# One PSUM pool from the projections to the end of attention, the first head's transposes inside the last gate block, roots shared by two token tiles, and `x` loaded ahead of the final additions

## The chip, the cores and the metric

The kernel runs on one core of one Trainium2 chip. TensorE (PE) does matmuls and transposes, VectorE (DVE), ScalarE (ACT) and GpSimd (POOL) the rest; SyncE (SP) and ScalarE issue the DMAs. The metric is the device time of one execution, in microseconds.

## The reference, cut to what matters

One layer of a hybrid encoder, sequence 1024, width 1024, batch 1, fp32. A Hyena branch (short convolution, two long convolutions with filters that a small MLP makes, 512 wide) and an attention branch (8 heads, 96 wide for q and k, 64 for v) are gated, added and multiplied by `w_out`:

```
h = rms_norm(x, g_norm); proj = h @ w_in
hy_in, z_hy, c_q, c_kv, k_rope, z_attn, gate_hy, gate_attn = split(proj)
v_h, x1, x2 = split(short_conv(hy_in))
k_spec = hyena_filter_spectra(...)          # sin(freq*(z @ w_f1 + b)), again with w_f2, then @ w_f3, decay, rfft
for o, gate in enumerate((x1, x2)):  zc = gate * long_conv(zc, k_spec[:, o], hy_bias[o])
u_hy = (zc * silu(z_hy)) @ w_hy_out
q = rms_norm(rms_norm(c_q) @ w_uq); kv = rms_norm(c_kv) @ w_ukv; k = rms_norm([k_nope, k_rope])   # rotary on 32 columns
u_attn = (softmax(q k^T / sqrt(96)) v * silu(z_attn)) @ w_attn_out
g_hy, g_at = split(sigmoid([gate_hy, gate_attn] + b_gate))
out = x + (g_hy * u_hy + g_at * u_attn) @ w_out
```

## The kernel before

Each fp32 product is made of three matmuls over operands split into a high and a low part (`hh`, `hl` are the two parts of the normalised input, transposed; `wh`, `wl` those of a weight block). The order of the instructions on each engine comes from a list scheduler of the framework with a cost model of its own; tiles come from pools with a number of buffers for each tag, and a tile that takes a buffer waits until the readers of the one before are done.

The stages, as TensorE goes through them: the startup (`build_hT`: transposes `ptx` of the normalised rows `xs`, in two halves of four row tiles, evacuated into `hh`, `hl`); the filter MLP (`pf`, with sines on ScalarE and many VectorE operations, two column halves); filter spectra (`pk`, `pu`) up to about 212 us; two long convolutions (`pu`, `pi`) up to about 605; `qkv` up to about 685; the last gate blocks up to 719; attention from there to 976 in 64 units (`S` scores, `pt` transposes of the exponentials `pr`, `pv` products with v); the two branch outputs (`hyena_out`, `pmo`); and the tail, the product with `w_out` in seven block products (`prod`, `po`) up to 1142.

Projections run all through this: 41 blocks of `proj_block`, each 48 matmuls `pm`, besides one of `proj_rope`; the scheduler lays them as fillers between the others. One block has two column halves of 512 in two PSUM banks (tag `mm`, 4 buffers), and each is evacuated by an instruction of its own: a sigmoid into `ob` for a gate (`fill_g`), copies for the latents (`fill_c`) and the short convolutions (`short_block`), sigmoid and product for `fill_z`. The PSUM pool `pp` closes before attention, whose scores, transposes and `pv` have pools of their own (`ssp`, `asp`).

`qkv` makes q, k and v for eight token tiles, two by two. For each tile it sums squares, takes a root with `rsqrt` (12 VectorE operations, three of them line L157), multiplies q and k by it, and stores them in DRAM (`qd`, `kdr`, `vd`); q and k have 4 buffers each. `load_pair` loads them back as `qr`, `kr`, `vr`, and the first head's 16 transposes (`pth`, function `prep`) turn them into `qh`, `ql`, `kh`, `kl`. Behind these loads in SP's queue stand five loads of `w_hy_out` tiles into `wr`, which ScalarE casts to `wh`.

In the tail, `finish(r, c, i, u, ps)` issues the load of an `x` tile (`xr`, 3 buffers), lets GpSimd add `u` (L1064), VectorE the product `ps` (L1065), and stores the tile; loads and stores of all 16 tiles stand in SP's queue in this order.

Of the kernel before, what the change touches and what calls it, by code (L numbers as in the profile page):

```python
# [34 lines left out]
CVB, MMB = 2, 4  # L35
# [58 lines left out]
class K:  # L94
# [106 lines left out]
    def build_hT(self, hp, xp):  # L201
# [6 lines left out]
        bank = lambda t: self.pp.tile([P, 512], F32, tag=t, bufs={"mm": MMB, "tp": 2, "cv": CVB}[t], name=self.nm("ptx"))  # L208
# [66 lines left out]
    def filter_mlp(self, fp, f1):  # L275
# [15 lines left out]
        for c in range(2):  # L291
            sl = slice(c * 512, (c + 1) * 512)
            self.split(z2[:, sl], zh[:, sl], zl[:, sl], after=self.half0)
            ps = self.pp.tile([P, 512], F32, tag="cv", bufs=CVB, name=self.nm("pf"))
            self.mm3(ps, w1h, w1l, zh[:, sl], zl[:, sl], True, True)
            x = self.sin_layer(f1, ps, fv[:, 0:1], fv[:, 1:2], 512)
            self.split(x, h1h[:, sl], h1l[:, sl])
        for c in range(2):
            sl = slice(c * 512, (c + 1) * 512)
            ps = self.pp.tile([P, 512], F32, tag="cv", bufs=CVB, name=self.nm("pf"))  # L300
# [27 lines left out]
    def filter_spectra(self, wk):  # L328
# [4 lines left out]
        for o in range(2):  # L333
            for hf in range(NHALF):
# [5 lines left out]
                for tp in range(4):  # L340
# [3 lines left out]
                    for d in range(2):  # L344
                        ps = self.pp.tile([P, 2, CW], F32, tag="cv", bufs=CVB, name=self.nm("pk"))
# [84 lines left out]
    def leaf_fwd(self, k, r, ch, cl, take):  # L430
# [5 lines left out]
        ps = self.pp.tile([P, 2, CW], F32, tag="cv", bufs=CVB, name=self.nm("pu"))  # L436
# [11 lines left out]
    def leaf_inv(self, k, p):  # L448
# [5 lines left out]
        ps = self.pp.tile([P, 2, CW], F32, tag="cv", bufs=CVB, name=self.nm("pi"))  # L454
# [97 lines left out]
    def proj_block(self, c0, m=P):  # L552

        nc, wp = self.nc, self.wp
        ps = [self.pp.tile([P, 512], F32, tag="mm", bufs=MMB, name=self.nm("pm")) for _ in range(2)]
        src = self.a["w_in"][0].rearrange("(d p) c -> p d c", p=P)
        for g in range(2):
# [5 lines left out]
            for i in range(4):  # L563
                d = 4 * g + i
                for (w, h, f) in ((wh, self.hh, 0), (wh, self.hl, 1), (wl, self.hh, 2)):
                    for c in range(2):
                        nc.tensor.matmul(ps[c][0:m], lhsT=w[:, i, 0:m], rhs=h[d][:, c * 512:(c + 1) * 512],  # L567
                                         start=(d == 0 and f == 0), stop=(d == 7 and f == 2))
        return ps

    def proj_rope(self, c0):

        nc, wp = self.nc, self.wp
        ps = [self.pp.tile([P, 512], F32, tag="mm", bufs=MMB, name=self.nm("pm")) for _ in range(2)]
# [6 lines left out]
        for d in range(8):  # L581
            for f, h in enumerate((self.hh, self.hl)):
                for c in range(2):
                    nc.tensor.matmul(ps[c][0:64], lhsT=w[:, d], rhs=h[d][:, c * 512:(c + 1) * 512],
                                     start=(d == 0 and f == 0), stop=(d == 7 and f == 1))
        return ps

    def short_block(self, blk, ps):
# [5 lines left out]
        for c in range(2):  # L594
            nc.scalar.copy(out=raw[:, 1 + c * 512:1 + (c + 1) * 512], in_=ps[c])
# [37 lines left out]
    def xz(self, b):  # L633
# [4 lines left out]
        for c in range(2):  # L638
            sl = slice(c * 512, (c + 1) * 512)
            nc.scalar.activation(out=sg[:, sl], in_=ps[c], func=AF.Sigmoid)  # L640
            nc.vector.tensor_tensor(out=sg[:, sl], in0=sg[:, sl], in1=ps[c], op=ALU.mult)
            nc.vector.tensor_tensor(out=acc[:, sl], in0=acc[:, sl], in1=sg[:, sl], op=ALU.mult)
# [4 lines left out]
    def fill_c(self, b):  # L647
# [4 lines left out]
        for c in range(2):  # L652
            nc.scalar.copy(out=ob[0:m, c * 512:(c + 1) * 512], in_=ps[c][0:m])
# [13 lines left out]
    def fill_z(self, b):  # L667
# [3 lines left out]
        for c in range(2):  # L671
            sl = slice(c * 512, (c + 1) * 512)
            nc.scalar.activation(out=ob[:, sl], in_=ps[c], func=AF.Sigmoid)
            nc.vector.tensor_tensor(out=ob[:, sl], in0=ob[:, sl], in1=ps[c], op=ALU.mult)
        nc.sync.dma_start(out=self.zaT[b], in_=ob)

    def fill_g(self, b):
        nc = self.nc
        ps = self.proj_block(3232 + b * P, P)
        ob = self.op.tile([P, L], F32, tag="ob", bufs=3, name=self.nm("ob"))  # L680
        for c in range(2):
            sl = slice(c * 512, (c + 1) * 512)
            nc.scalar.activation(out=ob[:, sl], in_=ps[c], func=AF.Sigmoid, bias=self.bg[:, b:b + 1])
# [9 lines left out]
    def convs(self, hf):  # L693
# [14 lines left out]
        for i in range(NB):  # L708
# [3 lines left out]
            for g in range(2):  # L712
                ps = self.pp.tile([P, 4, P], F32, tag="cv", bufs=CVB, name=self.nm("pty"))
# [7 lines left out]
    def qkv(self, kp):  # L721
# [56 lines left out]
        for hf in range(4):  # L778
            if hf < 3:
                C.update({(hf + 1, i): latent(hf + 1, i) for i in range(5)})  # L780
            ch, cl = [C[hf, i][0] for i in range(5)], [C[hf, i][1] for i in range(5)]
            for j in range(2):
# [55 lines left out]
    def attention(self, yp, wp, ssp, sp):  # L838
# [5 lines left out]
        rt = wp.tile([P, 512], F32R, tag="rT", name="rT")  # L844
        nc.gpsimd.memset(rt[64:P].bitcast(F32), 0.0)
        W = 2 * P

        def prep(h, j):
# [5 lines left out]
            if c == 0:  # L854
                QK[h, n] = [wp.tile([96, L], F32R, tag=n + x, bufs=2, name=self.nm(n + x)) for x in "hl"]
# [6 lines left out]
            if j == 3:  # L862
# [18 lines left out]
        def soft(u):  # L881
# [6 lines left out]
            pr = wp.tile([P, L], F32, tag="pr", bufs=2, name=self.nm("pr"))  # L888
# [376 lines left out]
```

## Time and profile before

| | |
|---|---|
| median of 3 runs | 1156.49 us (1154.57 to 1156.57) |
| profiled execution | 1155.32 us, span 1153.4 us |
| TensorE | busy 1099.4 us (95%), 5525 matmuls, mean granted clock 0.988 |
| VectorE, ScalarE, GpSimd | 893.0 (77%), 589.4 (51%), 107.3 us (9%) |
| chain that ended last | PE 65%, DVE 14%, DMA 10%, ACT 6%, issue 3% |

The span is the time from the first to the last instruction; 1.9 us of the execution lie outside it. A busy share is an average over all stages. The clock is the granted share of 2.4 GHz, 1.00 at full speed and 0.50 at 1.2 GHz, so that a mean between them is a mixture of the two. "Idle" in a row is the time that the engine waited just before, with what ended it.

### The profile page before, as it was taken

To read this page: it belongs to the slowest core of one execution; us is meant where nothing else is said; L and a number is where in the kernel's file an instruction comes from. 1 tells how busy PE (TensorE), PEld (TensorE's weight loads), DVE (VectorE), ACT (ScalarE), POOL (GpSimd) and SP (SyncE) were. 2 spreads that over 40 slices of the span, in tenths; PEclk is the share of its full clock that TensorE was granted. 3 is DMA by queue.
4 is the path that set the end of the run, shared out by engine and by line. 5 is a ranking of instruction groups with operands and counts; after the bars stand their busy time and mean duration, and the time that the engine had idled before them with its cause. 6 is when DMAs were issued, how large, how long until landed. Compare 5 with 4: busy or idle time off the path is not lost.

```text
span 1153.4 us, 15529 instructions
## 1 busy us (share of the span) xinstructions
PE 1099.4 (95%) x5525; PEld 909.7 (79%) x5525; DVE 893.0 (77%) x1631; ACT 589.4 (51%) x1101; POOL 107.3 (9%) x112
## 2 busy tenths in 40 slices
PE   4899999999999999999999999999999999999996
PEld 3678888888888888878887887787888887778874
DVE  6988788698788886778774893789788888478882
ACT  6745555754445434433433852777877776322420
POOL 0000000000000000000000132102200000250353
PEclk9989999999999999999999999899999999999998
DMA  5446444642335334334227557402202001896345
GB/s 212 133 146 198 155 163 174 205 119 65 89 91 147 105 115 128 91 88 127 91 83 233 148 154 248 146 29 74 92 25 77 1 20 50 274 298 217 91 128 182
DMA packets 119221, 150.27 MB, mean 130 GB/s; under 512 B 8548, under 2 KB 82408, under 8 KB 119144
## 3 DMA queue, kind: packets, MB, share of 16 engines
q1 hardware_dynamic: 107688, 120.97, 34.1%
q10 hardware_dynamic: 11456, 28.32, 6.6%
q8 instruction: 43, 0.70, 0.3%
q14 instruction: 34, 0.28, 0.1%
HBM read 101.81 MB, written 47.45 MB: 129 GB/s over the span
## 4 chain that ended last, share of the span: by engine, by line
PE 65%; DVE 14%; DMA 10%; ACT 6%; issue 3%; POOL 1%; SPq 0%; ACTq 0%; POOLq 0%; DVEq 0%
PE pm L567 33%; PE pu L128 8%; PE pt L903 4%; PE pi L128 4%; DMA wor<-in_w_out_dram 3%; PE S L119 2%; PE S L122 2%; PE S L121 2%; ACT pr L889 2%; PE pv L915 2%; PE pv L916 2%; DVE gg L988 1%; DMA out_dram<-xr 1%; DVE mo L139 1%; ACT PTh L138 1%
## 5 line engine op out<-in xcount | busy, mean ns | idle before, releaser
L567 PE MATMUL pm<-hh,wh 128*128 128x512 f32 x656 | 208.6, 393 | 1.8 <-DVE hl L143 0.9
L567 PE MATMUL pm<-hl,wh 128*128 128x512 f32 x656 | 208.9, 393 | 0.0
L567 PE MATMUL pm<-hh,wl 128*128 128x512 f32 x656 | 208.3, 392 | 0.1
L567 PEld LDWEIGHTS pm<-hh,wh 128*128 128x128 f32 x656 | 123.1, 189 | 27.7 <-DVE hl L143 1.1
L567 PEld LDWEIGHTS pm<-hh,wl 128*128 128x128 f32 x656 | 123.2, 188 | 26.0 <-DVE wl L139 0.5
L567 PEld LDWEIGHTS pm<-hl,wh 128*128 128x128 f32 x656 | 123.0, 188 | 25.3
L138 ACT CAST wh<-wr 128x512 fp32r<-128x512 f32 x98 | 60.3, 621 | 158.1 <-PE pm L567 107.7
L138 ACT CAST PTh<-pt 128x512 fp32r<-128x512 f32 x128 | 72.8, 587 | 41.1 <-PE pt L903 39.6
L139 DVE TENSOR_TENSOR PTl<-pt,PTh 128x512 fp32r<-128x512 f32 x128 | 83.8, 682 | 10.8 <-ACT PTh L138 10.2
L887 DVE TENSOR_REDUCE mx<-S 128x1 f32<-128x1024 f32 x64 | 77.9, 1217 | 13.2 <-PE S L122 13.1
L139 DVE TENSOR_TENSOR wl<-wr,wh 128x512 fp32r<-128x512 f32 x95 | 66.8, 708 | 15.7 <-ACT wh L138 15.4
L903 PE MATMUL pt<-ident,pr 128*128 128x128 f32 x512 | 75.9, 278 | 2.4 <-DVE PTl L139 1.4
L889 ACT ACTIVATE pr<-S,mx 128x1024 f32<-128x1024 f32 x64 | 71.8, 1121 | 7.0 <-DVE mx L887 6.6
L903 PEld LDWEIGHTS pt<-ident,pr 128*128 128x128 f32 x512 | 59.3, 142 | 18.2 <-DVE PTl L139 4.7
L915 PE MATMUL pv<-PTh,vc 128*128 128x256 f32 x256 | 69.1, 297 | 0.4 <-DVE at L926 0.4
L916 PE MATMUL pv<-PTl,vc 128*128 128x256 f32 x256 | 67.9, 293 | 0.0
L473 DVE TENSOR_TENSOR t<-pu,kt 128x512 f32<-128x512 f32 x64 | 41.0, 681 | 31.3 <-PE pu L128 30.7
L138 ACT CAST rh<-res 128x512 fp32r<-128x512 f32 x64 | 39.5, 619 | 41.8 <-PE pu L128 20.5
L119 PE MATMUL S<-kh,qh 96*128 96x512 f32 x128 | 54.5, 426 | 2.4 <-ACT pr L889 2.3
L121 PE MATMUL S<-kh,ql 96*128 96x512 f32 x128 | 53.5, 418 | 0.0
L122 PE MATMUL S<-kl,qh 96*128 96x512 f32 x128 | 52.5, 410 | 0.0
L915 PEld LDWEIGHTS pv<-PTh,vc 128*128 128x128 f32 x256 | 48.5, 189 | 4.7 <-DVE at L926 1.9
(285 smaller groups left out, 2391.2 us busy)
## 6 DMA issues: line engine op xcount, KB each, us to landing
wr<-in_w_in_dram SPq DMA_DIRECT2D x82, 256.0 KB, 3.2
wor<-in_w_out_dram SPq DMA_DIRECT2D x36, 256.0 KB, 4.7
dec<-in_dec_dram SPq DMA_DIRECT2D x16, 512.0 KB, 3.6
gT<-ob ACTq DMA_DIRECT2D x16, 512.0 KB, 2.9
gg<-gT SPq DMA_DIRECT2D x16, 512.0 KB, 4.4
kd<-kt ACTq DMA_DIRECT2D x28, 256.0 KB, 2.3
kt<-kd SPq DMA_DIRECT2D x28, 256.0 KB, 2.7
m<-gg ACTq DMA_DIRECT2D x16, 256.0 KB, 4.3
```

What stands on the lines that cost most here:

```text
L119: m = nc.tensor.matmul(out, lhsT=lh, rhs=rh, start=start, stop=False)
L121: nc.tensor.matmul(out, lhsT=ll, rhs=rh, start=False, stop=False)
L122: nc.tensor.matmul(out, lhsT=lh, rhs=rl, start=False, stop=stop)
L128: m = self.nc.tensor.matmul(out, lhsT=x, rhs=y, start=n == 0, stop=n == len(ops) - 1)
L138: self.behind(self.nc.scalar.copy(out=hi, in_=x), after)
L139: (eng or self.nc.vector).tensor_tensor(out=lo, in0=x, in1=hi.bitcast(F32), op=ALU.subtract)
L567: nc.tensor.matmul(ps[c][0:m], lhsT=w[:, i, 0:m], rhs=h[d][:, c * 512:(c + 1) * 512], start=(d == 0 and f == 0), stop=(d == 7 and f == 2))
L887: nc.vector.tensor_reduce(out=mx, in_=ps, axis=AX.X, op=ALU.max, negate=True)
L889: i = nc.scalar.activation(out=pr, in_=ps, func=AF.Exp, bias=mx, accum_out=RS[h // 2][:, qb, h % 2:h % 2 + 1])
L903: nc.tensor.transpose(out=pt[:, i], in_=pr[:, kb * P:(kb + 1) * P], identity=self.ident)
L915: nc.tensor.matmul(pv, lhsT=V[h][:, kb], rhs=hi[:, kb], start=(kb == 0), stop=False)
L916: nc.tensor.matmul(pv, lhsT=V[h][:, kb], rhs=lo[:, kb], start=False, stop=(kb == 7))
```

## The change

It has four parts.

1. PSUM. A block of `proj_block` or `proj_rope` takes one tile of two banks (tag `mm`, 2 buffers), and one instruction of 1024 columns evacuates it. The pool `pp` lives until attention is done, and the scores take the `mm` tiles too. The tiles with tag `cv` move to a pool `pc` of their own, which closes behind `qkv`; `pv` comes from a new pool `pa`.
2. Roots. Two token tiles share one root of 12 VectorE operations; `sqq` gets 2 buffers.
3. Seam. `attention` calls the last 16 block functions itself. The last gate block gets `mid`, a function called between its two weight groups: the first head's transposes. The casts of v come behind it (`vsplit`).
4. Tail. `fetch` loads `x` tiles ahead (6 buffers), ordered behind the last load of `w_out`; `plus` has GpSimd add `u` before the product; `finish` only adds the product and stores. The last four stores alternate between ScalarE's and SP's queue. `m1r` gets buffers of its own.

The diff, cut to its core:

```
-CVB, MMB = 2, 4
+CVB, MMB = 2, 2
...
+            if not two:
+                x = self.pp.tile([P, 2, 512], F32, tag="mm", bufs=MMB, name=self.nm("ptx"))
+                two.extend((x[:, 1], x[:, 0]))
+            return two.pop()
...
-    def proj_block(self, c0, m=P):
+    def proj_block(self, c0, m=P, mid=None):
...
-        ps = [self.pp.tile([P, 512], F32, tag="mm", bufs=MMB, name=self.nm("pm")) for _ in range(2)]
+        ps = self.pp.tile([P, 2, 512], F32, tag="mm", bufs=MMB, name=self.nm("pm"))
...
-                        nc.tensor.matmul(ps[c][0:m], lhsT=w[:, i, 0:m], rhs=h[d][:, c * 512:(c + 1) * 512],
+                        nc.tensor.matmul(ps[0:m, c], lhsT=w[:, i, 0:m], rhs=h[d][:, c * 512:(c + 1) * 512],
                                          start=(d == 0 and f == 0), stop=(d == 7 and f == 2))
-        return ps
+            if g == 0 and mid is not None:
+                mid()
+        return ps.rearrange("p a b -> p (a b)")
...
-    def fill_g(self, b):
+    def fill_g(self, b, mid=None):
...
-        for c in range(2):
-            sl = slice(c * 512, (c + 1) * 512)
-            nc.scalar.activation(out=ob[:, sl], in_=ps[c], func=AF.Sigmoid, bias=self.bg[:, b:b + 1])
+        nc.scalar.activation(out=ob, in_=ps, func=AF.Sigmoid, bias=self.bg[:, b:b + 1])
         nc.scalar.dma_start(out=self.gT[b], in_=ob)
...
+            ssq = kp.tile([P, 2, 2, 8], F32, tag="ssq", bufs=2, name=self.nm("ssq"))
+            QK = []
             for j in range(2):
...
-                rr = self.rsqrt(kp, ssq, 1.0 / 96, [P, 2, 8], "n2")
+                QK.append((tt, q, k))
+            r2 = self.rsqrt(kp, ssq, 1.0 / 96, [P, 2, 2, 8], "n2")
+            for j, (tt, q, k) in enumerate(QK):
+                rr = r2[:, j]
                 nc.vector.tensor_tensor(out=q, in0=q, in1=rr[:, 0].unsqueeze(2).broadcast_to([P, H, 96]), op=ALU.mult)
...
-            ps = ssp.tile([P, L], F32, tag="S", bufs=2, name=self.nm("S"))
+            ps = sp.tile([P, 2, 512], F32, tag="mm", bufs=MMB, name=self.nm("S")).rearrange("p a b -> p (a b)")
...
-        for j in range(4):
-            prep(0, j)
+        for f in fill[:-1]:
+            f()
+        fill[-1](lambda: [prep(0, j) for j in range(4)])
+        wp = room()
+        vsplit(0)
...
-        def finish(r, c, i, u, ps):
-            t = tp.tile([P, 512], F32, tag="xr", bufs=3, name=self.nm("xr"))
-            nc.sync.dma_start(out=t, in_=a["x"][0, r * 512 + i * P:r * 512 + (i + 1) * P, c * 512:(c + 1) * 512])
-            g_.tensor_tensor(out=t, in0=t, in1=u, op=ALU.add)
...
+        def fetch(r, c):
+
+            for i in range(4):
+                X[r, c, i] = t = tp.tile([P, 512], F32, tag="xr", bufs=6, name=self.nm("xr"))
+                t_, c_ = rows(r, c, i)
+                self.behind(nc.sync.dma_start(out=t, in_=a["x"][0, t_, c_]), self.lastw)
+
+        def plus(r, c, i, u):
+            g_.tensor_tensor(out=X[r, c, i], in0=X[r, c, i], in1=u, op=ALU.add)
+
+        def finish(r, c, i, ps, q=nc.sync):
+            t = X.pop((r, c, i))
+            t_, c_ = rows(r, c, i)
             v.tensor_tensor(out=t, in0=t, in1=ps, op=ALU.add)
...
+            q.dma_start(out=self.out[0, t_, c_], in_=t)
...
+        fetch(1, 1)
...
+            plus(1, 1, i, U3[i])
             ps = prod(S1, WT1, i)
             v.tensor_tensor(out=U2[i], in0=U2[i], in1=ps, op=ALU.add)
-            finish(1, 1, i, U3[i], ps)
+            finish(1, 1, i, ps)
+            if i == 0:
+                fetch(0, 1)
         for i in range(4):
-            finish(0, 1, i, U2[i], prod(S4, W22, i))
+            plus(0, 1, i, U2[i])
+        for i in range(4):
+            finish(0, 1, i, prod(S4, W22, i), (nc.scalar, nc.sync)[i % 2])
...
+    k.rp = srp.enter_context(k.pool("rp"))
+    aq = srp.enter_context(k.pool("aq"))
+    pa = pps.enter_context(k.pool("pa", space=PSUM))
...
+    fill = [lambda b=b: k.fill_z(b) for b in range(4)] + [lambda mid=None, b=b: k.fill_g(b, mid) for b in range(GEARLY, 16)]
```

How the order moves at three places (a number in a name tells the buffers apart). First TensorE's in the startup, between the transposes of the first row tiles and those of the second half (`ptx` from `xs_276` on, `xs_277` in the new order). Before, the first and the last rows of 24 `pm` of one column half, with seven transposes among them:

```order
L230 MATMUL ptx_203<-ident,xs_195 128x128
L567 MATMUL pm_1564<-hh_139,wh_1568 128x512
L567 MATMUL pm_1564<-hl_147,wh_1568 128x512
L567 MATMUL pm_1564<-hh_139,wl_1569 128x512
L567 MATMUL pm_1564<-hh_140,wh_1568 128x512
L567 MATMUL pm_1564<-hl_148,wh_1568 128x512
L567 MATMUL pm_1564<-hh_140,wl_1569 128x512
L567 MATMUL pm_1564<-hh_141,wh_1568 128x512
L567 MATMUL pm_1564<-hl_149,wh_1568 128x512
```

And now, at the same place:

```order
L241 MATMUL ptx_247<-ident,xs_198 128x128
L578 MATMUL pm_1565<-hh_142,wh_1568 128x512
L578 MATMUL pm_1629<-hh_142,wh_1632 128x512
L241 MATMUL ptx_285<-ident,xs_277 128x128
L241 MATMUL ptx_286<-ident,xs_277 128x128
L241 MATMUL ptx_299<-ident,xs_277 128x128
L241 MATMUL ptx_306<-ident,xs_277 128x128
```

Two `pm` stand there instead of 24; the others follow behind the second half's transposes. Counted over the whole order, 112 `pm` stand before the first `pk` instead of 96, 151 instead of 112 before the third, 214 instead of 171 before the first `pu`, 491 instead of 484 before the last `pu` of the spectra (between the two groups of the last set 7 instead of 28), and 576 before the first convolution in both. ScalarE's order holds eight table loads instead of seven, the added one among the sines of the filter MLP.

Second ScalarE's order at the seam, from the last gates to the first exponential. Now (before, the rows of `qh` and `kh` stood behind both halves of the last `ob`, and so behind the last `pm`):

```order
L688 ACTIVATE ob_6969<-pm_6908,cols 128x1024
L689 DMA gT_88<-ob_6969 128x1024
L138 CAST wh_9901<-wr_9899 128x512
L142 ACTIVATE qh_7003<-pth_7005,gq 96x512
L142 ACTIVATE qh_7003<-pth_7012,gq 96x512
L142 ACTIVATE kh_7019<-pth_7021,cols 96x512
L142 ACTIVATE kh_7019<-pth_7028,cols 96x512
L688 ACTIVATE ob_7065<-pm_6972,cols 128x1024
L689 DMA gT_89<-ob_7065 128x1024
L138 CAST vc_7085<-vr_6234 128x8x64
L138 CAST vc_7333<-vr_6234 128x8x64
L902 ACT_TABLE_LOAD
```

`wh_9901` is the cast of the third `w_hy_out` tile. On TensorE the four transpose groups now stand 24, 24, 19 and 17 `pm` before the end of the block, and the scores follow the last `pm`.

Third SP's queue at the end of the program. Before:

```order
L1063 DMA xr_11314<-in_x_dram 128x512
L1063 DMA xr_11332<-in_x_dram 128x512
L1066 DMA out_dram<-xr_11295 128x512
L1066 DMA out_dram<-xr_11314 128x512
L1063 DMA xr_11350<-in_x_dram 128x512
L1066 DMA out_dram<-xr_11332 128x512
L1063 DMA xr_11368<-in_x_dram 128x512
L1063 DMA xr_11386<-in_x_dram 128x512
L1066 DMA out_dram<-xr_11350 128x512
L1066 DMA out_dram<-xr_11368 128x512
L1066 DMA out_dram<-xr_11386 128x512
```

And now:

```order
L1101 DMA out_dram<-xr_11023 128x512
L1092 DMA xr_11116<-in_x_dram 128x512
L1101 DMA out_dram<-xr_11089 128x512
L1101 DMA out_dram<-xr_11091 128x512
L1092 DMA xr_11118<-in_x_dram 128x512
L1092 DMA xr_11120<-in_x_dram 128x512
L1101 DMA out_dram<-xr_11093 128x512
L1101 DMA out_dram<-xr_11095 128x512
L1101 DMA out_dram<-xr_11116 128x512
L1101 DMA out_dram<-xr_11120 128x512
```

The last load of `x` (`xr_11120`) stands ahead of four stores, where before it stood behind all but three.

## Rows read from the trace of the kernel before

**Rows 1.** The page: TensorE's busy time, share of the span, instructions, then the other engines.
```profile
PE 1099.4 (95%) x5525; PEld 909.7 (79%) x5525; DVE 893.0 (77%) x1631; ACT 589.4 (51%) x1101; POOL 107.3 (9%) x112
```

**Rows 2.** Stretches: length; busy us (x instructions) of PE, PEld, DVE, ACT, POOL; clock; DMA.
```profile
60.00:75.00 15.00, 14.54 (x69) 12.19 (x68) 11.32 (x20) 3.64 (x7) 0.00 (x0) 0.84 0.58 175
75.00:212.00 137.00, 137.00 (x669) 114.21 (x668) 116.56 (x239) 75.23 (x162) 0.28 (x4) 1.00 0.50 167
...
720.00:730.00 10.00, 8.04 (x28) 5.57 (x28) 4.12 (x5) 7.21 (x11) 4.59 (x5) 0.68 0.76 243
730.00:740.00 10.00, 10.00 (x55) 8.65 (x54) 7.40 (x9) 6.46 (x13) 0.00 (x0) 0.81 0.27 108
```

**Rows 3.** TensorE's waits: total us, times, longest.
```profile
PE pk L348 <- DVE h L306: 5.9, 1, 5.9
PE pq L119 <- ACT q L794: 3.2, 2, 1.8
...
PE pth L858 <- ACT ob L683: 1.7, 1, 1.7
PE po L119 <- DVE u L1152: 1.4, 1, 1.4
```

**Rows 4.** Timeline of TensorE in the startup, first and last of 24 `pm`: start, length.
```profile
22.17 0.50 PE L567 MATMUL pm<-hh,wh 128*128 128x512 f32 x1 [0.91 <-DVE hl L143]
...
28.45 0.39 PE L567 MATMUL pm<-hh,wl 128*128 128x512 f32 x1
```

**Rows 5.** Groups of ScalarE's instructions, and one line of VectorE (ns min/median/max).
```profile
L889 ACT ACTIVATE pr<-S,mx 128x1024 f32<-128x1024 f32 x64 | 71.8, 1121 | 7.0 <-DVE mx L887 6.6
...
L683 ACT ACTIVATE ob<-pm,cols 128x512 f32<-128x512 f32 x32 | 20.8, 682 | 17.2 <-PE pm L567 17.2
...
L157 DVE SCALAR_TENSOR_TENSOR rt<-rt,rv x36: 155/167/176, 13.4 to 699.4; 128x16 f32<-128x16 f32 x24, 128x4 f32<-128x4 f32 x6, 128x8 f32<-128x8 f32 x6
```

**Rows 6.** Timeline of ScalarE at four places, and VectorE's first maximum.
```profile
53.52 1.28 ACT L261 ACT_TABLE_LOAD   x1
...
670.54 1.05 ACT L794 ACTIVATE q<-pq,ry 128x384 f32<-128x384 f32 x2 [2.15 <-DMA qd<-q]
...
719.28 0.62 ACT L138 CAST wh<-wr 128x512 fp32r<-128x512 f32 x1 [3.27 <-DMA wr<-in_w_hy_out_dram]
...
728.77 1.11 ACT L889 ACTIVATE pr<-S,mx 128x1024 f32<-128x1024 f32 x1 [1.96 <-DVE mx L887]
...
727.51 1.22 DVE L887 TENSOR_REDUCE mx<-S 128x1 f32<-128x1024 f32 x1 [1.22 <-PE S L122]
```

**Rows 7.** Timeline of SP's queue: the last stores of q, the loads of `w_hy_out`.
```profile
698.09 0.36 SPq L818 DMA_DIRECT2D qd<-q  x1
...
703.32 0.36 SPq L818 DMA_DIRECT2D qd<-q  x1
...
707.78 10.50 SPq L977 DMA_DIRECT2D wr<-in_w_hy_out_dram  x4
```

**Rows 8.** Timeline of TensorE at the seam, and its last matmul.
```profile
718.22 0.61 PE L567 MATMUL pm<-hh,wl 128*128 128x512 f32 x2
720.54 1.08 PE L858 MATMUL pth<-ident,qr 128*96 128x128 f32 x8 [1.71 <-ACT ob L683]
723.04 1.75 PE L858 MATMUL pth<-ident,kr 128*96 128x128 f32 x8 [1.42 <-DVE ql L143]
...
730.03 1.97 PE L903 MATMUL pt<-ident,pr 128*128 128x128 f32 x8
...
1141.99 0.39 PE L122 MATMUL po<-wol,mo 128*128 128x512 f32 x1
```

**Rows 9.** The chain that ended last, in order of time: start, length, what.
```profile
1142.19 3.46 DMA out_dram<-xr
...
1145.66 2.67 DMA xr<-in_x_dram
...
1149.79 0.69 DVE xr L1065
```

More of the change, by code (lines that the diff above doesn't have):

```diff
@@ L651, in fill_c @@
         ob = self.op.tile([P, L], F32, tag="ob", bufs=3, name=self.nm("ob"))
[L652 to L653 removed]
+        nc.scalar.copy(out=ob[0:m], in_=ps[0:m])
         nc.scalar.dma_start(out=self.cT[b][0:m], in_=ob[0:m])
@@ L836, in load_pair, with attention @@
         return i
-    def attention(self, yp, wp, ssp, sp):
+    def attention(self, yp, aq, pa, fill, room):
         nc, a = self.nc, self.a
@@ L1214, in hyena_mla_kernel @@
-    with k.pool("gp2", side="right") as g2:
-        k.ah = [g2.tile([P, L], F32R, tag=f"ah{i}", name=f"ah{i}") for i in range(4)]
-        k.al = [g2.tile([P, L], F32R, tag=f"al{i}", name=f"al{i}") for i in range(4)]
-        with k.pool("ssp", space=PSUM) as ssp, k.pool("asp", space=PSUM) as sp, k.pool("awp") as wp:
-            k.mb = 1
-            k.attention(yp, wp, ssp, sp)
-            k.hyena_out(yp, sp, range(HSPLIT))
-        srp.close()
-        with k.pool("tps", space=PSUM) as pp, k.pool("tlp") as tp:
-            k.mb = 8
-            k.hyena_out(yp, pp, range(HSPLIT, 8))
-            k.tail(yp, g2, tp, pp)
+    pps, sr, srp = ExitStack(), ExitStack(), ExitStack()
@@ new lines, in hyena_mla_kernel @@
+    k.pp = pps.enter_context(k.pool("pp", space=PSUM))
+    hp = sr.enter_context(k.pool("hp", side="right"))
+    k.wp = sr.enter_context(k.pool("wp", side="right"))
+    k.op = sr.enter_context(k.pool("op", side="right"))
+    with k.pool("pc", space=PSUM) as k.pc:
+        with k.pool("fp") as fp:
+            with k.pool("xp") as xp, k.pool("fp1") as f1:
+                k.setup(xp)
+                k.load_x(xp, 0)
+                k.load_x(xp, 1)
+                k.filter_loads(f1)
+                k.build_hT(hp, xp)
+                k.filter_mlp(fp, f1)
+                k.selection()
+            svw = ExitStack()
+            k.vw = svw.enter_context(k.pool("vw", side="right"))
+            with k.pool("fpb") as fb:
+                k.filter_tables(fb)
+                with k.pool("fwk") as wk:
+                    k.filter_spectra(wk)
+                    for b in range(GEARLY):
+                        k.fill_g(b)
+        with k.pool("uq") as k.uq, k.pool("gp") as gp, k.pool("vb") as k.vb:
+            k.proj_vx(0)
+            k.load_gu(gp)
+            k.convs(0)
+            k.proj_vx(1)
+            k.convs(1)
+        svw.close()
+        for b in range(6):
+            k.fill_c(b)
+        with k.pool("kp") as kp:
+            k.qkv(kp)
@@ new lines, in hyena_mla_kernel, with room @@
+    yp = ctx.enter_context(k.pool("yp"))
+    k.rp = srp.enter_context(k.pool("rp"))
+    aq = srp.enter_context(k.pool("aq"))
+    pa = pps.enter_context(k.pool("pa", space=PSUM))
+    k.raw = {}
+    k.load_pair(0)
+    k.hyena_tiles(yp)
+    fill = [lambda b=b: k.fill_z(b) for b in range(4)] + [lambda mid=None, b=b: k.fill_g(b, mid) for b in range(GEARLY, 16)]
+    g2 = []
+    def room():
+        sr.close()
+        g2.append(ctx.enter_context(k.pool("gp2", side="right")))
+        k.ah = [g2[0].tile([P, L], F32R, tag=f"ah{i}", name=f"ah{i}") for i in range(4)]
+        k.al = [g2[0].tile([P, L], F32R, tag=f"al{i}", name=f"al{i}") for i in range(4)]
+        return srp.enter_context(k.pool("awp"))
@@ L1228 @@
+    k.mb = 1
+    k.attention(yp, aq, pa, fill, room)
+    k.hyena_out(yp, pa, range(HSPLIT))
+    srp.close()
+    pps.close()
+    with k.pool("tps", space=PSUM) as pp, k.pool("tlp") as tp:
+        k.mb = 8
+        k.hyena_out(yp, pp, range(HSPLIT, 8))
+        k.tail(yp, g2[0], tp, pp)
 _INS = ["x", "w_in", "w_f3", "hy_bias", "w_hy_out", "w_uq", "w_ukv", "g_qn", "g_kn", "w_attn_out", "w_out"]
```

138 lines of the change are left out of this document (54 added, 84 removed).

## Prediction

> **What bounds the kernel now.** The page's first part comes first: TensorE is busy 95% of a span of 1153.4 us [rows 1]. The work on it hardly changes, so the time can fall only where TensorE waits, where its clock is low, or after its last matmul. The list of its waits gives the first: 5.9 us where the first spectra matmul (`pk`) waits for the filter MLP, 3.2 us in `qkv`, 1.7 us at the first head's transposes, 1.4 us in the tail [rows 3]. The table by stretches gives the second: 2.4 GHz nearly everywhere, but a mean of 0.84 from 60 to 75, 0.68 from 720 to 730 and 0.81 from 730 to 740, each behind one of these waits [rows 2]. The third is the tail: the last matmul starts at 1141.99 and is over at 1142.4, 11.0 us before the span ends [rows 8].
>
> The profiled execution took 1155.3 us, 1.9 more than its span and 1.2 below the median of 1156.5. I sum against 1155.3. I take 0.2% of the time (2.3 us) as what a measurement here can tell from no change.
>
> **1. The tail: -7.4.** The chain that ended last runs, from 1142.19, over a store (3.46), the `x` load that stood behind it in SP's queue (2.67), POOL's addition, and VectorE's addition at 1149.79 [rows 9]. The matrix product was over all the time. Afterwards `x` is fetched up to six tiles ahead and POOL adds U before the products, so that after the last matmul only VectorE's addition of 0.69 us and the last store are left. That store is 1153.4 - 1150.48 = 2.9 us in the trace. So T + 0.1 + 0.7 + 2.9 = T + 3.7 instead of T + 11.0: -7.3, and with the last four stores on two queues -7.4. Bounds: the next to last store still under way adds its 3.46, so -4; and if the same untangling of the queue also ends the wait of 1.4 [rows 3], -8.8. What is late next: the four last `x` tiles need buffers that earlier stores free. By the order the last fetch stands behind the stores of tiles one product group earlier, and a product is 12 matmuls of 0.23 us, so a group of four lasts 11 us, against store plus load of 3.46 + 2.67 = 6.1 [rows 9]. That fits.
>
> **2. The seam to attention: -5.5.** Before, the last gate matmul starts at 718.22 and is over at 718.8; the first 8 transposes wait to 720.54, the others to 723.04, and the first `pt` comes at 730.03 [rows 8]: 11.2 us. In between TensorE does 16 transposes (1.08 us for the first eight) and two score units of 6 matmuls. A matmul of 512 columns adds 0.23 us (two take 0.61, one 0.39 [rows 4, 8]). Afterwards the 16 transposes lie inside the last block, with 17 `pm` behind them. The end of that block moves to 718.8 + 2 x 1.08 = 721.0. Then come S0 (6 x 0.23 = 1.4), the rest of its last matmul (0.39 - 0.23 = 0.2), the maximum (1.22), the exponential (1.11) [rows 6] and two hops of 0.05: `pt` at 725.0, so -5.0. S1 fills 1.4 of the wait, and some 1.2 us of idling stay there. The table load hides behind S0 and the maximum. Of the clock: over 730 to 740 TensorE was busy 10 us at 0.81 [rows 2], which is 1.9 us lost. If the shorter wait does not lower it, -6.9; if it is lowered as before, -5.0. I take -5.5.
>
> The Trainium skill (TensorE: Matmul & The Clock Gate, Part 1: The HAM clock gate) says that TensorE's clock goes to its lower level when it idles and comes back only after sustained work. By that rule the idling that stays would lower it again, and the sum would be by 1.9 us worse than by a clock that stays up.
>
> Bounds of the seam: -6.9, and +0.5 if a wait takes the place (rival C).
>
> **3. Startup and spectra: +1.** Both column halves of a block now share one PSUM tile, and the order keeps the writes of a tile in line. The 24 half-block matmuls that TensorE did from 22.17 to 28.45 while the rows of x were normalised [rows 4] shrink to two, since the other half of `hT` is not there yet: 22 x 0.23 = 5.0 us of idling added. On the other side the order puts 112 `pm` before the first `pk` instead of 96. Where TensorE had run dry lie now the 22 moved and 16 more, 38 x 0.23 = 8.7 us: the 5.9 us wait [rows 3] is filled, and the first `pk` starts 2.8 us later but 16 matmuls (3.7 us) ahead: -0.8 in all, the early idling included. Without the wait there is less reason for the low clock of 60 to 75, 15 us at 0.84 or 2.4 us [rows 2]; the new idling near 25 may cost as much, so I count half, -1.2. At the other end, before the last spectra `pu` tiles stand 7 fillers instead of 28, because 43 have been spent earlier and both orders have 576 when the first convolution starts. If that stretch's chain through VectorE stays as long as it was, TensorE idles 21 x 0.23 = 4.8 us; VectorE is busy 117 of 137 us there [rows 2], near its limit, so I count more than half: +3. Sum -0.8 - 1.2 + 3 = +1. Bounds: -3.2 (the clock wins 2.4, no idling) and +6.0 (4.8, and 1.2 of clock lost).
>
> ScalarE gets one more table load here, eight in the order instead of seven; a load takes 1.28 us [rows 6] and stands ahead of a sine of the MLP, whose second half then comes later; 39 `pm` stand there in the order, so nothing is added on TensorE. If that cover were gone, 1.3.
>
> The Trainium skill (ScalarE: Activation LUTs, What ACT_TABLE_LOAD costs) counts 2.66 us for each switch, a load and a drain. The trace shows the load alone; by the page the uncovered price would be 2.7 instead of 1.3.
>
> **4. Shared roots: 0.** Four roots fewer of 12 VectorE operations of 0.17 us [rows 5] are 48 x 0.17 = 8 us of VectorE, which is not the bound. What is late: the first of two tiles waits for the second one's sum of squares, so its q is multiplied and stored later. ScalarE waited 2.15 us at 670.54 for a store of q to free a buffer, and TensorE up to 1.8 [rows 3, 6]. The first q store of a pair comes later by up to the spacing of two tiles (698.09 to 703.32, 5.2 [rows 7]), the second right behind it and so earlier than before. One wait grows, the next one goes; I put 0, bounds -3.2 (both q waits vanish) and +15 (rival D). Behind the last matmul of `qkv`, VectorE's chain loses one such spacing of 5.2 and a root of 2: the last q store, now at 703.32, comes by my estimate 7 us earlier. Nothing on TensorE's path wants it until the seam.
>
> **5. Evacuations by one instruction: 0.** A gate's sigmoid of 512 columns takes 682 ns, an exponential of 1024 takes 1121 [rows 5]. So 42 blocks save about 0.24 us each, 10 us of a ScalarE that is busy 51%. In the cover of the fillers that is nothing; if an evacuation held up a pair, the two pairs would show it as `pm` waiting for `ob`.
>
> **Sum.** -7.4 - 5.5 + 1 + 0 + 0 = -11.9; 1155.3 - 11.9 = 1143.4. Measured against the median it would be 1144.6. I put 1144.
>
> **The rivals.**
> A. As summed, 1144, with a range of 1140 to 1148. Chance 0.50.
> B. Startup and spectra give back the most: +6 instead of +1, 1149. For it: VectorE is at 85% there, and the order has no fillers left. Against it: TensorE is busy 137.00 of the 137 us from 75 to 212 [rows 2]. Chance 0.15.
> C. The seam stalls on a load. On ScalarE the cast of the third `w_hy_out` tile stands ahead of the `qh` cast in the new order. In the trace this cast waited 3.27 us for its DMA, to 719.28 [rows 6], because the loads begin only at 707.78, behind the last q store [rows 7]. `tp` has two buffers, so the third transpose group would wait for the casts, and the 17 `pm` behind it: seam +0.5, total 1149.5. Against it: if the stores end 7 us sooner, the tile lands near 712.3, and the transposes are due 24 `pm` before the end, at 718.8 - 5.5 = 713.3. A margin of 1 us. Chance 0.15.
> D. Slower: the q buffers. If for each of three pairs of tiles TensorE waits a cycle of 6 us (the spacing of 5.2 and a hop or two) instead of the 3.2 us in all [rows 3], `qkv` loses 18 - 3 = 15 us, 1158.5. Against it: the order stores the second tile sooner than before. It decides from 5 us a pair on. Chance 0.06.
> E. The tail doesn't do what it says: the fetches, ordered behind the last `w_out` load, come too late and the products' PSUM tiles fill up. Then the tail gains 2 instead of 7.4, 1149. Against it: the store and load of 6.1 us above. Chance 0.04.
> F. Everything helps: no idling in the last spectra set, the clock up at both places, the q waits gone: -8.8 - 6.9 - 3.2 - 3.2 = -22.1, and half of it beyond the sum already 1138. So 1133 to 1140. Chance 0.10.
>
> **Numbers.** Faster by over 0.2% (below 1154.2): A, B, C, E, F, less a tail of two of them meeting, 0.88. Within: 0.06. Slower (above 1158.8): most of D and one unknown, 0.06. The range 1137 to 1153 holds A, B, C, E and most of F.
>
> **What would show it.** The step in the tail: the last matmul about 3.7 us before the end, with no VectorE wait for POOL there. The seam: `pt` some 4.0 us behind the last `pm`, the transposes without waits, and the third `w_hy_out` cast before 713. The startup: idling near 25, no 5.9 us wait, and new waits of `pu` for VectorE near 205. In `qkv`, waits on q below 4 us in all. I am wrong if TensorE's new waits before 680 come to more than 10 us.

## The result: slower by 0.6%

The changed kernel took 1163.01 us (median of 4 runs, 1160.68 to 1163.38), the kernel before 1155.53 in the same sessions (1152.77 to 1156.57): a ratio of 1.0061, 95% interval 1.0044 to 1.0077. The sign of the forecast was wrong. The profiled execution took 1162.93 us, its span is 1161.1, 7.7 longer than the span before.

The page after: TensorE, VectorE, ScalarE and GpSimd do about what they did [rows 1], with 41 instructions fewer on ScalarE and 60 fewer on VectorE.

```profile
PE 1099.5 (95%) x5525; PEld 907.0 (78%) x5525; DVE 893.1 (77%) x1571; ACT 584.9 (50%) x1060; POOL 108.7 (9%) x112
```

TensorE's waits after (total, times, longest). The 5.9 us of `pk` and the 1.7 of `pth` for `ob` [rows 3] are gone. New are the 5.0 of `pth` for `ql` (1.4 before [rows 8]), the waits of `ptx` and `pm` in the startup, and those of `pu`: four in the spectra, and the 1.6 for `gt` in the convolutions, at 444.58.

```profile
PE pth L867 <- DVE ql L143: 5.0, 1, 5.0
PE pq L119 <- ACT q L800: 4.4, 3, 2.0
PE pu L128 <- ACT rh L138: 4.1, 2, 2.0
...
PE po L119 <- DVE u L1189: 2.5, 1, 2.5
PE pm L578 <- ACT wh L138: 2.4, 1, 2.4
PE ptx L241 <- DVE hl L143: 2.3, 1, 2.3
...
PE pu L128 <- DVE gt L721: 1.6, 1, 1.6
...
PE pu L128 <- ACT kt L378: 1.2, 1, 1.2
PE pu L128 <- DVE rl L139: 1.1, 2, 0.9
PE pu L128 <- ACT rh L453: 0.8, 1, 0.8
```

Stretches after, columns as in [rows 2], with one more, 190 to 210. The low clock of 60 to 75 is cured; from 22 to 60 it is 0.91 instead of 0.97. From 75 to 212 TensorE is no longer busy throughout; in 190 to 210 VectorE is busy without a gap, TensorE 15.11 of 20 us at 0.91.

```profile
60.00:75.00 15.00, 15.00 (x77) 12.77 (x76) 8.23 (x14) 8.39 (x11) 0.00 (x0) 1.00 0.75 246
75.00:212.00 137.00, 131.86 (x638) 108.25 (x636) 118.29 (x234) 67.65 (x140) 0.41 (x6) 0.99 0.49 163
...
190.00:210.00 20.00, 15.11 (x70) 11.71 (x68) 20.00 (x38) 9.50 (x19) 0.13 (x2) 0.91 0.45 149
...
720.00:730.00 10.00, 4.97 (x27) 3.92 (x26) 1.32 (x2) 4.03 (x6) 4.30 (x4) 0.83 0.55 179
730.00:740.00 10.00, 9.68 (x38) 7.41 (x36) 3.08 (x5) 4.08 (x6) 1.23 (x2) 0.82 0.21 75
```

Where the time went: when the same matmul starts in the two profiled executions (us, read from the timelines of TensorE).

| | before | after | later by | its part |
|---|---|---|---|---|
| first `pk` | 58.86 | 61.81 | 2.95 | 16 `pm` (3.7) are ahead: -0.7 net |
| first `pi` of the first convolution | 243.88 | 251.88 | 8.00 | startup and spectra +8.00, or +7.5 net of 2 `pm` |
| last `pq` | 683.09 | 692.32 | 9.23 | convolutions, `qkv` +1.23 |
| first `pt` | 730.03 | 742.10 | 12.07 | seam +2.84 |
| 300th matmul of the scores | 913.47 | 924.93 | 11.46 | attention -0.61 |
| first `po` | 1063.41 | 1076.49 | 13.08 | `hyena_out` +1.62 |
| last `po` | 1141.99 | 1156.51 | 14.52 | products +1.44 |
| end of span | 1153.4 | 1161.1 | 7.7 | tail -6.8 |

The seam after, on TensorE (first), and on ScalarE and VectorE (second). The transposes of q run at 722.25; those of k wait 5.03 us for `ql`, since `tp` has two buffers. ScalarE stood 2.83 us at the cast `wh`, whose load came late, and `qh` starts behind it at 727.90. The first maximum is there at 739.50, but the exponential starts at 740.84, behind the table load.

```profile
722.25 1.03 PE L867 MATMUL pth<-ident,qr 128*96 128x128 f32 x8
...
729.48 1.09 PE L867 MATMUL pth<-ident,kr 128*96 128x128 f32 x4 [5.03 <-DVE ql L143]
...
736.21 0.62 PE L578 MATMUL pm<-hh,wl 128*128 128x512 f32 x2
...
742.10 1.09 PE L916 MATMUL pt<-ident,pr 128*128 128x128 f32 x8 [2.42 <-ACT pr L902]
```

```profile
727.38 0.62 ACT L138 CAST wh<-wr 128x512 fp32r<-128x512 f32 x1 [2.83 <-DMA wr<-in_w_hy_out_dram]
727.90 1.25 ACT L142 ACTIVATE qh<-pth,gq 96x512 fp32r<-96x512 f32 x2
...
738.27 1.23 DVE L900 TENSOR_REDUCE mx<-S 128x1 f32<-128x1024 f32 x1 [4.49 <-PE S L122]
...
739.55 1.28 ACT L902 ACT_TABLE_LOAD   x1
740.84 1.11 ACT L902 ACTIVATE pr<-S,mx 128x1024 f32<-128x1024 f32 x1
```

The end of the chain that ended last: a store, an `x` load behind it, GpSimd's addition, VectorE's. The matmuls now last until 1156.9, 4.2 us before the end instead of 11.0 [rows 8, 9]. The last row, from VectorE's timeline, is the same addition with what it waited for.

```profile
1147.99 3.46 DMA out_dram<-xr
...
1151.47 2.71 DMA xr<-in_x_dram
...
1157.06 0.69 DVE xr L1100
...
1157.06 0.69 DVE L1100 TENSOR_TENSOR xr<-xr,po 128x512 f32<-128x512 f32 x1 [0.71 <-POOL xr L1095]
```

### The profile page after: what moved, and what is told of

The parts are those of the page before. It is cut to its first block, busy times and chain, and to the rows that moved or that the text cites. A ratio compares the mean times of both kernels' runs of the same rounds, so it can differ in the third digit from the quotient of the medians.

```text
span 1161.1 us, 15435 instructions
## 1 busy us (share of the span) xinstructions
PE 1099.5 (95%) x5525; PEld 907.0 (78%) x5525; DVE 893.1 (77%) x1571; ACT 584.9 (50%) x1060; POOL 108.7 (9%) x112
## 4 chain that ended last, share of the span: by engine, by line
PE 71%; DVE 10%; DMA 8%; ACT 6%; issue 3%; POOL 1%; ACTq 0%; SPq 0%; POOLq 0%; DVEq 0%
PE pm L578 34%; PE pu L128 7%; PE pt L916 4%; PE pi L128 4%; ACT pr L902 2%; PE S L119 2%; DMA wor<-in_w_out_dram 2%; PE S L122 2%; PE S L121 2%; PE pv L928 2%; PE pv L929 2%; PE pmo L121 1%; PE pmo L119 1%; PE pmo L122 1%; PE pth L867 1%
## 5 line engine op out<-in xcount | busy, mean ns | idle before, releaser
L578 PEld LDWEIGHTS pm<-hh,wl 128*128 128x128 f32 x656 | 123.1, 189 | 25.9 <-DVE wl L139 0.9
L139 DVE TENSOR_TENSOR wl<-wr,wh 128x512 fp32r<-128x512 f32 x95 | 67.0, 708 | 21.0 <-ACT wh L138 19.6
```

Source lines behind the costliest of these rows:

```text
L139: (eng or self.nc.vector).tensor_tensor(out=lo, in0=x, in1=hi.bitcast(F32), op=ALU.subtract)
L578: nc.tensor.matmul(ps[0:m, c], lhsT=w[:, i, 0:m], rhs=h[d][:, c * 512:(c + 1) * 512], start=(d == 0 and f == 0), stop=(d == 7 and f == 2))
```

## The experiments

Ratios are to the kernel before, on the same chip. A profile is one execution, and can lie some us from the median of its kernel; verdicts go by the ratios, places by the profiles. Where two versions are compared in us without a ratio, it is by their medians, which come from different sessions.

**The tail alone**, on the kernel before: `fetch`, `plus`, the 6 buffers, the two queues, `m1r`.

```
-            finish(0, 1, i, U2[i], prod(S4, W22, i))
+            plus(0, 1, i, U2[i])
+        for i in range(4):
+            finish(0, 1, i, prod(S4, W22, i), (nc.scalar, nc.sync)[i % 2])
```

> Only the tail part of the change, on the kernel before. Theory: what comes after the last matmul falls from 11.0 to 3.7 us and nothing else moves, so about 7 us faster than before (about 1148.5 us). Rival: the x loads, queued behind the w_out loads, hold up the products (in the changed kernel a wait of 2.5 us stands where 1.4 us stood), so 4 to 6 us faster.

Measured: 1150.18, ratio 0.9955 (0.9935 to 0.9975). In its profile the last matmul is over at 1138.7, 3.7 us before the end at 1142.5, and VectorE's addition waits for it alone:

```profile
1138.33 0.39 PE L122 MATMUL po<-wol,mo 128*128 128x512 f32 x1
...
1138.82 0.69 DVE L1079 TENSOR_TENSOR xr<-xr,po 128x512 f32<-128x512 f32 x1 [0.72 <-PE po L122]
```

So this part gives 5.2 us by the ratio (2.9 to 7.5 by its interval) and about 7 by the place of the last matmul.

**The shared roots alone**, on the kernel before.

```
-                rr = self.rsqrt(kp, ssq, 1.0 / 96, [P, 2, 8], "n2")
+            r2 = self.rsqrt(kp, ssq, 1.0 / 96, [P, 2, 2, 8], "n2")
```

> Only the shared roots, on the kernel before. Theory: VectorE saves 8 us off the path; TensorE's waits in qkv stay within 2 us of 3.2, the last q store comes 2 to 3 us earlier, and as the seam is a chain behind that store, the time falls by 0 to 2 us. Rival: the first tile of a pair is stored later, q buffers come free later, TensorE waits 3 to 6 us more, slower by that.

Measured: 1155.47, 0.9995 (0.9979 to 1.0012): nothing. The last q stores are issued by 698.77 + 1.77 = 700.5, the last one before by 703.32 + 0.36 = 703.7 [rows 7]; 3.1 earlier, of which the last `pq` has 0.9 (682.20 for 683.09).

```profile
698.77 1.77 SPq L822 DMA_DIRECT2D qd<-q  x2
...
704.41 0.33 SPq L838 DMA_DIRECT2D qr<-qd  x1
```

**The pairs alone**, on the kernel before: tiles of two banks, evacuations of 1024 columns, the pool `pc`.

```
-        ps = [self.pp.tile([P, 512], F32, tag="mm", bufs=MMB, name=self.nm("pm")) for _ in range(2)]
+        ps = self.pp.tile([P, 2, 512], F32, tag="mm", bufs=MMB, name=self.nm("pm"))
```

> Only the first part of the change on the kernel before: pairs of banks with one evacuation, the cv tiles in a pool of their own; seam, roots and tail as before. The order up to the first convolution is that of the changed kernel (112, 214, 491, 576 matmuls at the landmarks). Theory: the last spectra set waits for VectorE, the first convolution starts 7 to 9 us later than before, and all of it arrives at the end: 1162 to 1165. Rival: the loss needs the other parts too (the wait at the seam is only where the time is lost), and pairs alone cost 0 to 3 us.

Measured: 1165.78, 1.0094 (1.0073 to 1.0115), 9.9 us slower. The first convolution starts at 253.35, the spectra wait as in the changed kernel, and the transposes wait 7.7 us although nothing has been moved into the last gate block:

```profile
PE pth L863 <- DVE ql L143: 7.7, 1, 7.7
...
PE pu L128 <- ACT rh L138: 4.1, 2, 2.0
```

This one part costs more than the whole change. It holds the shared tile and the single evacuation together; the two were not run apart.

**One gate block more kept for the early stages**, on the changed kernel: `GEARLY = 8` becomes 9. That puts 28 `pm` instead of 7 between the two groups of the last spectra set, and 624 instead of 576 before the first convolution, taken from those behind `qkv`.

> The changed kernel with nine instead of eight gate blocks available before the first convolution. Theory F: the last set of filter spectra was left without fillers because the new order had spent 43 pm earlier; the ninth block fills TensorE's 7.1 us of waits there and the clock does not fall, and since the block is taken from the end, where nothing had to be covered, the time falls by 7 to 9 us against the changed kernel (about 1155). Rival V: that stretch is bound by VectorE, busy all the time from 190 to 210; the block brings splits and an evacuation there too, and the stretch grows by what it gains: 0 to 2 us.

Measured: 1155.64, 0.9984 (0.9969 to 1.0): 7.4 us faster than the changed kernel, as theory F had it. TensorE is busy throughout again, clock 1.00:

```profile
75.00:212.00 137.00, 137.00 (x669) 113.89 (x668) 117.94 (x238) 68.46 (x143) 0.14 (x2) 1.00 0.49 166
190.00:210.00 20.00, 20.00 (x99) 16.73 (x98) 19.74 (x42) 11.05 (x23) 0.00 (x0) 1.00 0.43 157
```

But at the seam the transposes of q now wait for the load of q:

```profile
PE pth L867 <- DMA qr<-qd: 6.7, 1, 6.7
```

From the last `pq` (692.69) to these transposes (718.55) it takes 25.9 us here, and the fillers left behind `qkv` no longer cover it. So the end was not a place "where nothing had to be covered".

**The casts of `w_hy_out` behind the first head's k cast**, on the changed kernel.

```
+            i = self.gsplit(ps[0:96], gq if n == "q" else gk, hi[:, sl], lo[:, sl])
+            if h == 0 and j == 3:
+                self.kcast = i
...
+            self.split(r, wh, wl, nc.gpsimd if self.mb == 1 else nc.vector, self.kcast if self.mb == 1 else None)
```

> The changed kernel with the casts of the first w_hy_out tiles ordered on ScalarE behind the first head's casts of q and k. Theory L: the 5.0 us wait of the third transpose group is the cast's wait for its load; it vanishes, and with it some low clock, so 5 to 6.5 us faster than the changed kernel (about 1157). Rival: the stores and loads of q and k themselves are late, and the transposes wait for them instead: 0 to 2 us.

Measured: 1159.04, 1.003 (1.0014 to 1.0045), 4.0 less than the changed kernel, whose interval it just touches. `qh` now waits for the transposes, not behind a load, the transposes of k wait no more, and `pt` starts at 737.17 instead of 742.10. From the last `pq` (694.00) to `pt` it takes 43.2 us, in the changed kernel 49.8, before 46.9. The spectra's waits stay.

```profile
724.56 1.26 ACT L142 ACTIVATE qh<-pth,gq 96x512 fp32r<-96x512 f32 x2 [4.76 <-PE pth L867]
```

```profile
726.15 0.64 PE L867 MATMUL pth<-ident,kr 128*96 128x128 f32 x4
```

**Both of these together.**

> Nine gate blocks ahead and the casts behind, together, on the changed kernel. Theory Q: with the ninth block gone from the end, TensorE reaches the seam before the loads of q and k have landed (it waited 6.7 us for them with nine blocks alone); the casts are then no longer what is late, so no more than 0 to 2 us faster than nine blocks alone (about 1154 to 1156). Rival: the two gains add up, 11 us faster than the changed kernel (about 1151).

Measured: 1155.18, 0.9992 (0.998 to 1.0004): no better than the ninth block alone. The wait for `qr` (6.6 us) is the limit, and ScalarE's order behind it makes no difference here.

**The first gate block by column halves**, on the changed kernel, so that the early matmuls need only the first half of `hT`.

```
+        if halves:
+            for c in range(2):
+                for g in range(2):
+                    self.proj_mm(ps, ws, g, m, (c,))
```

> The changed kernel with the two column halves of the first gate block one after the other (the shared PSUM tile stays), so that some 18 matmuls can be done near 25 us again; the counts of fillers at every later landmark are the same. Theory: the two waits of 2.3 and 2.4 us near 25 go, 3 to 5 us faster than the changed kernel (about 1159). Rival: the filter MLP's chain on VectorE and ScalarE sets the first spectra matmul, so TensorE only waits there instead: 0 to 1 us.

Measured: 1166.73, 1.0095 (1.0068 to 1.0122): no gain. Of the two waits near 25 the 2.4 us of `pm` goes, the 2.3 of `ptx` stays. The first `pk` moves by 0.9 to 60.94, the `pu` waits are the same, and the MLP's `pf` waits 1.9 us for VectorE. The early idling was not what the spectra lack.

**Ninth block, casts and halves together.**

> As the run before, with the first gate block's halves one after the other too. Theory Q: what is won at the start moves the whole chain of q forward as well, so 3 to 4 us faster than the run before (about 1151). Rival: none of it arrives, as the wait for q grows by what the start wins.

Measured: 1156.27, 1.0 (0.9983 to 1.0017), with the same 6.6 us for `qr`: theory Q missed by 5 us, and nothing arrives, as the rival said.

**Single banks, with seam, casts and tail**: the changed kernel with two tiles per block, evacuations by half, roots per tile, and the PSUM pool closed before the scores.

```
-        ps = self.pp.tile([P, 2, 512], F32, tag="mm", bufs=MMB, name=self.nm("pm"))
+        ps = [self.pp.tile([P, 512], F32, tag="mm", bufs=MMB, name=self.nm("pm")) for _ in range(2)]
...
+        pps.close()
+        ssp = aps.enter_context(k.pool("ssp", space=PSUM))
```

> The tail and the seam without the shared PSUM tiles: single banks with their two evacuations, the pool closed before the scores, roots for each tile as before; the first head's transposes inside the last gate block, the w_hy_out casts behind them. The order up to qkv is that of the kernel before. Theory: the loss before attention was all from the pairs in the startup; the time before qkv's end is that of the kernel before, the seam is 3 to 5 us shorter and the tail 7, so 1144 to 1147, faster than both kernels. Rival: the scores wait for the last block's two sigmoids, since their pool takes its banks, and the seam wins nothing: 1148 to 1150.

Measured: 1148.69, 0.9926 (0.9906 to 0.9946), the time that the rival gave, though the seam is shorter. The order up to `qkv` is that of before, and no `pu` wait is in the list. The last `pm` is over at 717.4, `pt` comes 6.4 us behind it instead of 11.2 [rows 8], the transposes not between them any more:

```profile
716.80 0.61 PE L567 MATMUL pm<-hh,wl 128*128 128x512 f32 x2
718.55 0.50 PE L119 MATMUL S<-kh,qh 96*128 96x512 f32 x1 [1.13 <-ACT ob L685]
...
723.78 1.09 PE L910 MATMUL pt<-ident,pr 128*128 128x128 f32 x8 [2.22 <-ACT pr L896]
```

Part of this goes again: from the 13th to the 97th matmul of the scores it takes 50.97 us, before 49.35.

**The same, with the casts of v and `w_hy_out` behind the first exponential.**

```
-        soft(0)
+        self.kcast = soft(0)
+        vsplit(0, self.kcast)
```

> The version with single banks, tail and seam (the run e8), with the casts of v and of w_hy_out ordered behind the first exponential instead of behind the casts of k. Theory: the first exponential waited 1 us for these casts and the table load behind them; 1 to 2 us faster than that run (about 1147). Rival: the casts then delay the first transposed tiles or the products with v by as much: no change.

Measured: 1147.3, 0.9924 (0.9912 to 0.9936). `pt` waits 1.20 instead of 2.22 us, 5.3 behind the last `pm`, but the time is that of the version before it within the intervals. Both are faster than either kernel. Against the tail alone (0.9935 to 0.9975) the intervals touch, so the time that the seam adds to the tail is not shown; in this profile `pt` comes 43.2 us behind the last `pq` (682.85), before 46.9.

```profile
721.80 0.50 PE L119 MATMUL S<-kh,qh 96*128 96x512 f32 x1 [1.13 <-ACT ob L685]
...
726.01 1.09 PE L908 MATMUL pt<-ident,pr 128*128 128x128 f32 x8 [1.20 <-ACT pr L894]
```

## Why the prediction was wrong, step by step

The forecast of the sum was -11.9, the spans differ by +7.7. The 19.6 between them are 8.3 in the seam (+2.8 for -5.5), 7.0 in startup and spectra (+8.0 for +1), 3.7 in the stretches put at nothing (+1.23 - 0.61 + 1.62 + 1.44) and 0.6 in the tail. Rivals B and C came together, and each cost more than its price.

**Step 3, startup and spectra, failed by its size.** The start came out right: -0.7 for the first `pk` against -0.8, and the clock of 60 to 75 came back. In part that is luck: the idling near 25 grew by 3.8 us (2.3 + 2.4 + 0.5 for 0.9 + 0.5) and not by 5.0, while the clock from 22 to 60 fell from 0.97 to 0.91, which the -0.8 did not hold.

The last term, "+3" with a bound of 4.8, failed. I priced the 21 fillers missing in one place. What the runs showed is that the pairs make the order spend 43 fillers before the first `pu`, in stages where they gain little (0.7 us up to the first `pk`). The 7 that are left for the last set come at its end, from 217.37 on, so that 42 `pu` stand in a row where 27 `pm` stood among them before; that alone makes 27 x 0.23 = 6.2 instead of 4.8. And the stage left without them is bound by VectorE: it is busy 20.00 of 20 us there (19.62 in the kernel before, where fillers kept TensorE busy meanwhile), and the first convolution reaches its first `pi` at 251.88 without the fillers and at 251.69 with the ninth block's.

The `pu` waits come to 4.1 + 1.2 + 1.1 + 0.8 = 7.2 us, and the clock of 0.91 costs 20 x 0.09 = 1.8. That the pairs do it is shown from three sides: alone they cost 9.9 us, without them the wait is absent, and with the fillers put back it is gone as well. The net +7.5 lies beyond my bound of +6.0. Of the 8.2 between the first `pk` and the first convolution (7.5 + 0.7), waits and clock less the 2.4 regained from 60 to 75 explain 6.6. The other 1.6 fit the `pu` themselves: the same 228 are busy 55.36 us in this stretch, 50.80 before, 4.6 more, of which the clock's 1.8 is a part.

**Step 2, the seam, failed by rival C's mechanism**, at a price of +2.8 instead of its +0.5. The step that failed is the estimate, made in step 4, that the last q store would come 7 us earlier. The last two are issued from 708.63 to 710.33, against 703.68 before; with the last `pq` 9.2 us later, that is 9.2 - 6.6 = 2.6 earlier in relation to TensorE. The roots alone show the same (3.1 earlier, the last `pq` 0.9 earlier: 2.2). What the estimate left out shows on VectorE: behind a common root stand the products of both tiles, 7.1 us from the first product of q to the last (702.82 to 709.94), where before only one tile's stood behind its root, 3.4 us (699.86 to 703.28).

```profile
699.86 0.96 DVE L809 TENSOR_TENSOR q<-q,ry 128x768 f32<-128x768 f32 x1
...
703.00 0.28 DVE L826 TENSOR_TENSOR q<-m 128x128 f32<-128x128 f32 x1
```

```profile
702.82 2.68 DVE L818 TENSOR_TENSOR q<-q,ry 128x768 f32<-128x768 f32 x2
...
709.66 0.28 DVE L835 TENSOR_TENSOR q<-m 128x128 f32<-128x128 f32 x1
```

The loads of `w_hy_out` behind the stores therefore gave rival C its late cast, at 727.38 and not before 713:

```profile
708.63 1.70 SPq L827 DMA_DIRECT2D qd<-q  x2
713.81 0.33 SPq L843 DMA_DIRECT2D qr<-qd  x1
...
715.15 14.58 SPq L998 DMA_DIRECT2D wr<-in_w_hy_out_dram  x5
```

Moving that cast away gave 4.0 us back, and in its profile the stretch from the last `pq` to `pt` is 6.6 shorter (43.2 for 49.8), so this cause is shown. Without it the seam is at -3.8 against the kernel before, of the -5.5 forecast. A second miss is part of the rest: the table load did not hide behind S0 and the maximum. On ScalarE it stands behind the last sigmoid and the casts of v, and the exponential starts 1.3 us after the maximum; `pt` comes 5.3 us behind the last `pm` and not 4.0. The margin of 1 us that I called evidence against C was the difference of two estimates, each less certain than it. In the pairs alone the cast that waits for this load stands in front of the first `qh` too (there it waited 3.44 us, to 731.67). The idea of the seam itself held: `pt` comes 5.3 us behind the last `pm` in the changed kernel (736.8 to 742.10) and 6.4 or 5.3 in the versions with single banks, against 11.2.

The Trainium skill (TensorE: Matmul & The Clock Gate, Part 1: The HAM clock gate) says that the array's clock is held down by default and that activity releases it. In the changed kernel's trace the clock fell while TensorE idled 5.03 us for `ql`: 1.00 from 724 to 726, 0.50 from 728 to 730; the means are 0.83 and 0.82 for 720 to 730 and 730 to 740.

**Why curing both did not give -12.** With the ninth block the 6.7 us wait for `qr` takes the place of the spectra's. The fillers behind `qkv` also cover the store and load of q, 25.9 us from the last `pq` on. What the early stages get, this one lacks. My prediction said of the q stores that "nothing on TensorE's path wants it until the seam", and didn't price that chain with fewer fillers.

**Step 1, the tail, was right**: 4.2 us after the last matmul, 3.7 in the part alone, against 3.7 forecast; in time the part alone gave 5.2 (2.9 to 7.5) of the 7.4. It is the only part shown to gain by itself; the seam was not run without the others. One sign was missed: in the changed kernel VectorE's last addition does wait for GpSimd, whose last `x` load is only just in time. It starts at 1157.06, 0.2 us after the matmul's end at 1156.9; in the part alone it waits for the matmul.

**Step 4, the roots, was right as a cost** at 0 (0.9995), though TensorE's waits for q came to 4.4, not below 4. **Step 5**, the merged evacuations, I put at nothing: no `pm` waits for `ob`. ScalarE lost 4.5 us of work, not the 10 estimated: two sigmoids of 512 in a row overlap and take 1.26 us, not 2 x 0.68 (`ob` at 719.81 before), and one of 1024 takes 1.11.

The +1.6 in `hyena_out` and +1.4 in the products (`po` for `u`, 2.5 for 1.4) were not tested. By the medians the pairs alone cost 9.9 and the whole change without the tail some 7.5 + 5.2 = 12.7. The 2.8 between them are no check of the seam's +2.8: the intervals are about as wide, and the pairs alone already lose 4.0 there (from the last `pq` at 691.20 to `pt` at 742.12).

The test that I had set, new waits of more than 10 us before 680, is met: 7.2 of `pu` in the spectra, 2.4 of `pm` and 2.3 of `ptx` in the startup and the 1.6 of `pu` for `gt` at 444.58 come to 13.5. The list alone would mislead, since 5.9 us went in exchange and the low clock stands in no such list; the starts of the same matmul show the loss.

## What to carry to other kernels

Work that fills the gaps of a busy engine is a budget: when a change makes a scheduler spend some earlier, count what is left for each later stage, down to the last store and load that it has to hide, and price the stage by the engine that bounds it there. Joining two buffers into one saved an instruction here and coupled their schedules, so look at the order of the whole program and not at the evacuation. Before moving work up to a seam, look at what stands ahead of it in each engine's queue and on which transfer that waits: a margin smaller than the error of its two ends is no margin.

## What was unexpected of the hardware

A small VectorE instruction took six times as long beside one of GpSimd. Before, the shift of L153 on 128x16 took 0.175 us in the first of the eight `qkv` tiles, where GpSimd was idle, and 1.01 to 1.03 in the other seven, where GpSimd's product of k had begun 0.7 to 1.1 us ahead of it. Each of the seven ended 0.03 us behind the end of that product, here at 694.20 + 1.66:

```profile
649.59 0.17 DVE L153 TENSOR_SCALAR rt<-rv 128x16 int32<-128x16 int32 x1
...
694.20 1.66 POOL L814 TENSOR_TENSOR k<-k,ry 128x512 f32<-128x512 f32 x1 [4.57 <-DVE rv L152]
...
694.88 1.02 DVE L153 TENSOR_SCALAR rt<-rv 128x16 int32<-128x16 int32 x1
```

With the shared roots no shift runs beside GpSimd and none takes more than 0.182, and now q's product shows the long cases (median 1166 ns for 958, longest 1799 for 961):

```profile
L818 DVE TENSOR_TENSOR q<-q,ry x8: 947/1166/1799, 665.4 to 703.7; 128x768 f32<-128x768 f32 x8
```

So long cases did not go, they are in another instruction now.

And the clock of a seam is not given by the code alone. The tail's experiment leaves the seam as it was, and its clock from 720 to 730 was 1.00, where the kernel before had 0.68 [rows 2], though TensorE was busy for less of it (7.14 us for 8.04). The first unit's score matmuls start 0.43 us apart in the one profile and 0.23 in the other, and `pt` came 1.8 us earlier (728.26), of which 0.7 was there at the last `pq`. A difference of 1 us in the seam between two profiles therefore says nothing.
